# A decoder trunk with two attention branches: when the values of the sliding branch are transposed, and when the modulation row sums run

## The chip, the cores and the metric

The kernel runs on one core of one Trainium2 chip, in one launch. The metric is the device time of that launch in microseconds (us); less is better. Comparisons are made between medians of several runs on the same chip.

The core has several engines that run side by side, each with its own queue in order: TensorE (PE) multiplies matrices and transposes, VectorE (DVE) and ScalarE (ACT) do element-wise work, GpSimd (POOL) does small jobs and issues some transfers, SyncE (SP) issues most transfers. An engine waits at an instruction until the semaphores that it names have arrived, and everything behind it on that engine waits too.

## The reference

D_MODEL = 1024, 512 positions, one layer, fp32. In outline:

```python
cs = silu(c)
mod = cs @ w_ada + b_ada                      # 6 rows of 1024: shift1, scale1, gate1, shift2, scale2, gate2
h = rmsnorm(x, norm1_g) * (1 + scale1) + shift1
qa, ka, va, qd, kd, vd, ga, gd = split(h @ w_in)
out_a = sliding_window_attention(qa, ka, va)  # 8 heads of 64, 2 kv heads, window 128, sinks, ALiBi
out_d = diff_attention(qd, kd, vd)            # 4 heads: (softmax_1 - lam * softmax_2) @ v, then rmsnorm per head
merged = sigmoid(ga) * (out_a @ w_branch_swa) + sigmoid(gd) * (out_d @ w_branch_diff)
x = x + gate1 * (merged @ w_out)
h2 = rmsnorm(x, norm2_g) * (1 + scale2) + shift2
x = x + gate2 * conv_ffn(h2)                  # up, causal conv of width 3, gelu, gate, down
return rmsnorm(x, final_g)
```

The rows shift1 and scale1 of `mod` are needed at the very start. The other four (gate1, shift2, scale2, gate2) are needed after the attentions only.

## The kernel before

**Stages.** From 0 to about 60 us the kernel computes shift1 and scale1, the first norm and the first six column blocks of the projection. Then follow the sliding attention (60 to 125 us), the differential attention (125 to 225 us), the gates, branches, merge and output projection, and the MLP with its norm. An fp32 product is made of three fp32r matmuls (`mm3`, L118 to L121): each operand is split into a high part (a copy on ACT, L115 or L430) and a low part (a subtraction on DVE, L116 or L431).

**Order on PE.** The order of PE's work is written out by hand (`manual_schedule`). `fill(n)` (L495) puts n ticks of projection work between the steps of the attentions. A tick is one k slice of a projection: three 128x512 matmuls, 0.23 us each from start to start. `SWA_FILL` and `DIFF_FILL` say how many ticks go where. The order on DVE and ACT is chosen when the program is built, from priorities and estimated times; the softmaxes and the evacuations of transposes have a high one (`HP`). Once built, each engine keeps that order.

**Sliding attention.** Four pairs of heads; for pair i: `swa_scores(i, 0)` and `swa_scores(i, 2)` (first and last two blocks of 128 queries; L563 adds the bias and takes the row maxima on DVE), `swa_softmax` (exponentials on ACT, scaling L586 on DVE), `swa_transpose(i, 0)` and `(i, 1)` (L598, two groups each, every group into a bank of PSUM), `swa_values`. `turn_va` (L448) transposes the values of this branch on PE and evacuates them as high and low part.

**Differential attention.** 16 steps s = (h, n): head h, query block n, whose scores span (n + 1) x 128 keys. `diff_scores` (reductions L680), `diff_softmax` (exponentials L694, reciprocal L697, scalings L699, L700), `diff_transpose` (L709, evacuated to `aTh` and `aTl` by L430 and L431). The scores of blocks 0 and 1 of a head are made together, and their softmaxes are asked for one behind the other. At block 0 of the next head come the values of the head before (`diff_values`), and some ticks behind these the statistics of its norm (`pss`, `rt`, with a power on POOL at L175) and their spread (`rb`, L739, multiplied in by L740).

**The tag "t".** Two banks of PSUM with the tag "t" are shared in turn by `pva`, the transposes `tp`, `td` and `pv`, the norm's `pss` and `rb`, and the row's `pr`.

**The modulation rows.** `ada_rows` (L750) makes the four later rows in halves of 512, so eight of them, each in four steps. A step is one load of 512 KB (`ra`, L757, on SP's queue, in one of four buffers `raw` that weight loads share) and two sums on DVE (`arow`, L762 or L764: 128 x 512 times a column of `cs`, plus what is there). After the fourth step the sums are split (`arh` on ACT, `arl` on DVE, L116), and one tick later `ada_spread` adds up the 128 partitions by two matmuls on PE (`pr`), copies the row on ACT and writes it to memory by a transfer of POOL. The next row's first sum waits for that transfer, as the row has one buffer. `fill` takes a step at every eighth tick, from tick 8 on, whatever stage runs. After tick 20 (`ADA_EASY`) the sums have half of the high priority.

Of the kernel before, what the change touches and what calls it, by code (L numbers as in the profile page):

```python
# [11 lines left out]
ALU = mybir.AluOpType  # L12
# [15 lines left out]
HP = 100000  # L28
ST = 6
ADA_LAG = 1  # L30
ADA_EVERY = 8
ADA_EASY = 20
ADA_START = 4
V_LAG = 13
STAT_LAG = 10
NORM_LAG = 16
SWA_FILL = (2, 2, 5, 2, 2, 2, 2, 3)
# [16 lines left out]
def kernel(  # L54
# [22 lines left out]
    nc = tc.nc  # L77
# [15 lines left out]
    def fbank(name):  # L93
        return bank("f", 2, [P, S], name)
# [4 lines left out]
    def tbank(name, shape=(P, S)):  # L99
        return bank("t", 2, list(shape), name)  # L100
# [4 lines left out]
    def raw_tile(shape, name):  # L105
        return wp.tile(shape, F32, tag="raw", bufs=4, name=name)

    def split_pair(raw, shape, name):
        hi = wp.tile(shape, F32R, tag="whi", bufs=WB, name=name + "_h")
        lo = wp.tile(shape, F32R, tag="wlo", bufs=WB, name=name + "_l")  # L110
        split(hi, lo, raw)
        return hi, lo
# [314 lines left out]

    def evac(hi, lo, src, scale=None):
        if scale is None:
            nc.scalar.copy(hi, src)  # L430
            nc.vector.tensor_sub(lo, src, hi.bitcast(F32))  # L431
        else:
            nc.scalar.activation(hi, src, AF.Copy, scale=scale)
            nc.vector.scalar_tensor_tensor(lo, src, scale, hi.bitcast(F32), ALU.mult, ALU.subtract)
# [3 lines left out]
    def evac_q(i):  # L438
        evac(qa[:, i, 0], qa[:, i, 1], acc6[i], qsc[:, i : i + 1])
# [8 lines left out]
    def turn_va():  # L448
        pv = tbank("pva")
        for t in range(NT):  # L450
            nc.tensor.transpose(pv[:, t * P : (t + 1) * P], vT[:, t * P : (t + 1) * P], ident)
        pv3 = pv.rearrange("p (t d) -> p t d", t=NT)
        for a, cc in ((0, 0), (64, 192)):
            evac(va[:, 0, :, cc : cc + 64], va[:, 1, :, cc : cc + 64], pv3[:, :, a : a + 64])
# [20 lines left out]
    def load_cols(src, col, name):  # L475
        r = raw_tile([P, KT, P], name)
        nc.sync.dma_start(r, src[:, col : col + P].rearrange("(a p) n -> p a n", p=P))
        return split_pair(r, [P, KT, P], name)
# [9 lines left out]
    current, tick = [], [0]  # L488

    def prefetch():  # L490
        while units and len(loaded) < 2:
            load, run = units.pop(0)
            loaded.append((load(), run))

    def fill(n):  # L495
        for _ in range(n):
            if not current:
                prefetch()
                if loaded:
                    wts, run = loaded.pop(0)  # L500
                    current.append(run(wts))
                    if tick[0]:
                        prefetch()
            if tick[0] == 7:
                prefetch()
            if current:
                try:
                    next(current[0])
                except StopIteration:
                    current.clear()  # L510
            for e in list(later):
                e[0] -= 1
                if e[0] <= 0:
                    later.remove(e)
                    e[1]()
            tick[0] += 1
            if tick[0] >= ADA_START and tick[0] % ADA_EVERY == 0:
                next(ada, None)

    def after(n, fn):  # L520
        later.append([n, fn])

    def steps(o, wts, rhs, nk, k0=0, cl=slice(0, P)):
        wh, wl = wts
        for k in range(nk):
            mm3(o, wh[:, k, cl], wl[:, k, cl], rhs[0][k0 + k], rhs[1][k0 + k], k == 0, k == nk - 1)
            if k < nk - 1:
                yield
# [59 lines left out]
    def swa_transpose(i, j):  # L588
        c = pairs[i]
        ph = ap.tile([P, 1024], F32R, tag="aTh", bufs=2, name=f"pTh{i}_{j}")  # L590
        pl = ap.tile([P, 1024], F32R, tag="aTl", bufs=2, name=f"pTl{i}_{j}")
        for b in range(2):
            wb = 512 if b == 0 else 384
            tp = tbank(f"tp{i}_{j}_{b}")
            for m in range(wb // P):
                kb, n = 2 * b + m // 2, 2 * b + m // 2 + m % 2
                off = (kb - max(0, n - 1)) * P
                nc.tensor.transpose(tp[:, m * P : (m + 1) * P], c.sb[n][:, j, off : off + P], ident)  # L598
            with tc.high_priority(offset=HP):
                evac(ph[:, b * 512 : b * 512 + wb], pl[:, b * 512 : b * 512 + wb], tp[:, :wb])  # L600
        c.pT.append((ph, pl))

    def swa_values(i):
# [80 lines left out]
            scored[s] = mx, pm  # L684

    def diff_softmax(s):
        with tc.high_priority(offset=HP):
            h, n = divmod(s, NT)
            slope = 2.0 ** (-2 * (h + 1))
            mx, pm = scored[s]  # L690
            lsum = ap.tile([P, 2], F32, tag="dls", bufs=3, name=f"dls{h}_{n}")
            nc.vector.tensor_scalar_mul(mx, mx, -slope)  # L692
            for m in range(2):
                nc.scalar.activation(  # L694
                    pm[m], pm[m], AF.Exp, bias=mx[:, m : m + 1], scale=slope, accum_out=lsum[:, m : m + 1]
                )
            nc.vector.reciprocal(lsum, lsum)  # L697
            nc.vector.tensor_mul(lsum[:, 1:2], lsum[:, 1:2], nlam)
            nc.vector.tensor_scalar_mul(pm[1], pm[1], lsum[:, 1:2])  # L699
            nc.vector.scalar_tensor_tensor(pm[0], pm[0], lsum[:, 0:1], pm[1], ALU.mult, ALU.add)  # L700
            probs[s] = pm[0]

    def diff_transpose(s):
# [78 lines left out]
    def add_gate_a(j):  # L782
        def gate(wts):
            o = fbank(f"pga{j}")
            yield from steps(o, wts, hT, KT)
            nc.scalar.activation(ta[:, j], o, AF.Tanh, scale=0.5)

        def load():
            if j % 2 == 0:
                r = raw_tile([P, 4, 2 * P], f"wba{j}")  # L790
                for a in range(2):
                    nc.sync.dma_start(
                        r[64 * a : 64 * a + 64],
                        wba[256 * a : 256 * a + 256, j * P : (j + 2) * P].rearrange("(i p) n -> p i n", p=64),
                    )
                pair_w["a"] = split_pair(r, [P, 4, 2 * P], f"wba{j}")
            return pair_w["a"]

        def branch(wts):
            o = fbank(f"pA{j}")  # L800
            rhs = [[outa[b][:, k] for k in range(4)] for b in range(2)]
            yield from steps(o, wts, rhs, 4, cl=slice(j % 2 * P, j % 2 * P + P))
            nc.vector.scalar_tensor_tensor(ta[:, j], ta[:, j], 1.0, o, ALU.add, ALU.mult)

        units.append((lambda: load_cols(win, COL_GA + j * P, f"wga{j}"), gate))
        units.append((load, branch))

    pairs, firsts, scored, probs, aTs = {}, {}, {}, {}, {}
    ada = ada_rows()
    add_head(0)  # L810
    add_head(1)
    fill(SWA_FILL[0])
    swa_scores(0, 0)
    with tc.issue_after(pairs[0].last.ins):
        fill(SWA_FILL[1])
        swa_scores(0, 2)
    with tc.issue_after(pairs[0].last.ins):
        swa_softmax(0)
        fill(1)
        evac_q(3)  # L820
        turn_va()
        fill(SWA_FILL[2] - 1)
    for i in range(SWA_PAIRS):
        more = i + 1 < SWA_PAIRS
        if more:
            swa_scores(i + 1, 0)
        fill(SWA_FILL[3])
        swa_transpose(i, 0)
        fill(SWA_FILL[4])
        swa_transpose(i, 1)  # L830
        if more:
            swa_scores(i + 1, 2)
        fill(SWA_FILL[5])
        if more:
            swa_softmax(i + 1)
        fill(SWA_FILL[6])
        swa_values(i)
        fill(SWA_FILL[7])
# [11 lines left out]
    for s in range(4 * DIFF_HEADS):  # L850
        h, n = divmod(s, NT)
        if n == 0 and 0 < h < 3:
            add_head(h + 1)
        elif s == 12:
            add_gate_a(2)
            add_gate_a(3)
        fill(DIFF_FILL[1])
        nxt = {0: (), 1: (s + 1,), 2: (s + 1,), 3: (s + 1, s + 2)}[n] if s < 15 else ()
        if nxt:
            diff_scores(*nxt)  # L860
        fill(DIFF_FILL[2])
        diff_transpose(s)
        for z in nxt:
            diff_softmax(z)
        if n == 0 and h:
            diff_values(h - 1)
            fill(DIFF_FILL[3])
    for j in range(4, KT):
        add_gate_a(j)
    fill(1)  # L870
# [653 lines left out]
    e = cbuf[1][:, 1024:2048].rearrange("p (t n) -> p t n", n=S)  # L1524
# [269 lines left out]
```

## Time and profile before

| | |
|---|---|
| time, median of 3 runs | 715.93 us (714.68 to 716.32) |
| the profiled execution's own time | 716.59 us |
| its span in the trace | 714.5 us |
| mean granted clock of PE | 0.993 |
| PE busy | 688.4 us (96%) |
| weight loads of PE (PEld) | 603.0 us (84%) |
| DVE busy | 588.5 us (82%) |
| ACT busy | 384.2 us (54%) |
| row sums L764 | 56 of 748 ns, 41.9 us in all |
| loads `ra` | 32 of 512 KB, 4.2 us from issue to landing (median) |

How to read it: busy time is the time in which an engine has an instruction in work, and PE's matmuls are pipelined, so that one that is recorded as 0.39 us long starts 0.23 us after the one before. The span is shorter than the execution's time by 2.1 us, which lie around it. In a row of the timeline stand start, duration, engine, line, operation, out<-in, tile, shape, count, and in brackets how long the engine had been idle before and what released it. In windows and waits, idle time of an engine counts only where another waits for it.

### The profile page before, as it was taken

The numbers are of one execution on the slowest core, as the hardware profiler recorded it, in microseconds if no ns is written. First come the engines' busy times: TensorE is split into PE (matmuls) and PEld (weight loads), VectorE is DVE, ScalarE is ACT, GpSimd is POOL, SyncE is SP. The second block draws the span as 40 slices with busy tenths as digits, with TensorE's granted clock in tenths as the row PEclk, the third lists the DMA queues.
The fourth block names the chain that finished last, engine by engine and source line by source line (L and its number), as shares of the span: only waits on it lengthen the run. The fifth ranks groups of instructions, "written<-read, shape, count | busy, mean of one in ns | idle before, by whom it ended". The sixth has DMA issues, their size and how long they took to land. (4 is left out here: it accounts for less than half of the span.)

```text
span 714.5 us, 11275 instructions
## 1 busy us (share of the span) xinstructions
PE 688.4 (96%) x4187; PEld 603.0 (84%) x4187; DVE 588.5 (82%) x1125; ACT 384.2 (54%) x677; POOL 84.4 (12%) x101
## 2 busy tenths in 40 slices
PE   5999899999999999999999999999999999999994
PEld 5777778777787888888879999999999999888884
DVE  5998978797986774865479899888889899979996
ACT  3646566455554233432258666555555666656664
POOL 4000000001000100000012021111111102540300
PEclk9999999999999999999999999999999999999998
DMA  9983522453553664737717598877789738996903
GB/s 307 293 264 96 173 64 83 148 163 102 151 159 105 225 196 140 235 118 210 232 59 148 153 201 203 191 185 217 190 199 229 164 123 233 182 203 194 160 0 119
DMA packets 115863, 121.82 MB, mean 170 GB/s; under 512 B 4415, under 2 KB 93280, under 8 KB 115808
## 3 DMA queue, kind: packets, MB, share of 16 engines
q1 hardware_dynamic: 96894, 95.09, 42.1%
q0 software_dynamic: 18720, 25.73, 21.2%
q8 instruction: 33, 0.54, 0.3%
q10 hardware_dynamic: 194, 0.28, 0.1%
q14 instruction: 22, 0.18, 0.1%
HBM read 118.97 MB, written 2.11 MB: 169 GB/s over the span
## 5 line engine op out<-in xcount | busy, mean ns | idle before, releaser
L1133 PE MATMUL up<-t,m_whi 128*128 128x256 f32 x528 | 96.1, 283 | 0.0
L1133 PEld LDWEIGHTS up<-t,m_whi 128*128 128x128 f32 x528 | 82.3, 192 | 0.0
L1133 PE MATMUL up<-t,m_wlo 128*128 128x256 f32 x264 | 74.7, 283 | 0.1
L1133 PE MATMUL up<-bh,p_wlo 128*128 128x256 f32 x232 | 65.7, 284 | 0.6 <-DVE p_wlo L1076 0.6
L1133 PE MATMUL up<-bh,p_whi 128*128 128x256 f32 x232 | 65.6, 283 | 0.0
L1133 PE MATMUL up<-bl,p_whi 128*128 128x256 f32 x232 | 65.6, 283 | 0.0
L1133 PEld LDWEIGHTS up<-t,m_wlo 128*128 128x128 f32 x264 | 50.6, 192 | 0.3 <-DVE m_wlo L1076 0.3
L1133 PEld LDWEIGHTS up<-bh,p_wlo 128*128 128x128 f32 x232 | 44.4, 192 | 1.1 <-DVE p_wlo L1076 1.1
L1133 PEld LDWEIGHTS up<-bh,p_whi 128*128 128x128 f32 x232 | 44.5, 192 | 0.0
L1133 PEld LDWEIGHTS up<-bl,p_whi 128*128 128x128 f32 x232 | 44.5, 192 | 0.0
L1044 POOL DMA_DIRECT2D s<-in_w_up_dram x21 | 27.2, 1385 | 143.0 <-DMA s<-in_w_up_dram 92.7
L764 DVE SCALAR_TENSOR_TENSOR arow<-ra,cs,arow 128x512 f32<-128x512 f32 x56 | 41.9, 748 | 1.4 <-DMA ra<-in_w_ada_dram 0.7
L1076 DVE TENSOR_TENSOR m_wlo<-s,m_whi 128x1024 fp32r<-128x1024 f32 x31 | 37.7, 1216 | 2.0 <-ACT m_whi L1072 2.0
L1072 ACT CAST m_whi<-s 128x1024 fp32r<-128x1024 f32 x31 | 32.5, 1047 | 9.3 <-DVE s L1066 5.9
L1133 PE MATMUL up<-t,p_whi 128*128 128x256 f32 x176 | 32.2, 283 | 0.0
L175 POOL TENSOR_TENSOR r<-ms,mhalf 128x1 f32<-128x1 f32 (+1 forms) x16 | 13.4, 838 | 144.7 <-DVE ms L173 77.2
L694 ACT ACTIVATE sd<-sd,dmx 128x128 f32<-128x128 f32 (+3 forms) x32 | 17.8, 556 | 22.0 <-DVE dmx L692 15.4
L777 POOL DMA_DIRECT2D mod_rows<-arow x8 | 4.3, 540 | 200.5 <-ACT arow L776 200.3
L1133 PEld LDWEIGHTS up<-t,p_whi 128*128 128x128 f32 x176 | 27.4, 192 | 0.2 <-issue 0.2
L1140 ACT ACTIVATE gT<-a,cv 128x512 f32<-128x512 f32 x22 | 17.7, 813 | 17.6 <-DVE a L1175 17.3
L1072 ACT CAST p_whi<-wa 128x1024 fp32r<-128x1024 f32 x18 | 18.7, 1042 | 12.0 <-PE up L1133 10.8
L1133 PE MATMUL up<-t,p_wlo 128*128 128x256 f32 x88 | 24.9, 283 | 0.0
(485 smaller groups left out, 2119.5 us busy)
## 6 DMA issues: line engine op xcount, KB each, us to landing
ra<-in_w_ada_dram SPq DMA_DIRECT2D x32, 512.0 KB, 4.2
wa<-in_w_up_dram SPq DMA_DIRECT2D x22, 512.0 KB, 4.6
s<-in_w_up_dram SPq DMA_DIRECT2D x21, 512.0 KB, 5.0
s<-in_w_up_dram POOLq DMA_DIRECT2D x21, 512.0 KB, 6.5
adaw<-in_w_ada_dram SPq DMA_DIRECT2D x16, 512.0 KB, 5.1
w<-in_w_in_dram SPq DMA_DIRECT2D x12, 512.0 KB, 3.9
a<-in_w_up_dram SPq DMA_DIRECT2D x11, 512.0 KB, 4.7
b<-in_w_down_dram SPq DMA_DIRECT2D x10, 512.0 KB, 3.9
```

The costliest lines, as they stand in the source:

```text
L175: nc.gpsimd.tensor_tensor(r0, ms, mhalf[:, :n], ALU.pow)
L694: nc.scalar.activation(pm[m], pm[m], AF.Exp, bias=mx[:, m : m + 1], scale=slope, accum_out=lsum[:, m : m + 1])
L764: nc.vector.scalar_tensor_tensor(ac, r[:, a], cc, ac, ALU.mult, ALU.add)
L777: nc.gpsimd.dma_start(mod_rows[idx : idx + 1, hf * S : (hf + 1) * S], row)
L1044: nc.gpsimd.dma_start(dst, upblock(*blk), accum_op=ALU.add)
L1072: nc.scalar.copy(W[J, name][0], R[J, SRC[name]])
L1076: nc.vector.tensor_sub(lo, R[J, SRC[name]], hi.bitcast(F32))
L1133: nc.tensor.matmul(o[u], w[:, k, cu], b[:, k], start=name in ("p1", "m5", "p2") and k == 0 and x == 0, stop=k == 3 and x == 2, skip_group_ ...
L1140: nc.scalar.activation(grow(j), av[J][:, u], AF.Identity, bias=cv[:, 66 + j : 67 + j], scale=cv[:, 44 + j : 45 + j])
```

## The change

Three things are changed. First, `turn_va` stands between the two first score blocks of the sliding attention, one tick behind the first, where it stood behind the first softmax; the tick 7 prefetch of weights is replaced by one that is issued behind the first pair's transposed probabilities (`pairs[0].turned`, the copy on ACT). Second, the steps of `ada_rows` are held back until the differential attention: no step is taken while `hold` is set, which it is during the sliding attention and at the blocks n = 2 and 3 of a head. At n = 0 and 1 a step is taken every 4 ticks, and after the differential attention every 6. A step taken at a tick issues its load and enters its two sums into DVE's work; where these come in DVE's order is decided at the build. Third, the softmax of block 1 of a head is issued behind the last exponential and the last multiplication of block 0's (`issue_after`).

No matmul, transpose, sum or load is added or removed in number.

```diff
--- before.py
+++ after.py
@@ -28,9 +28,9 @@
 HP = 100000
 ST = 6
 ADA_LAG = 1
-ADA_EVERY = 8
+ADA_EVERY = 4
+ADA_LATE = 6
 ADA_EASY = 20
-ADA_START = 4
 V_LAG = 13
 STAT_LAG = 10
 NORM_LAG = 16
@@ -427,8 +427,9 @@
 
     def evac(hi, lo, src, scale=None):
         if scale is None:
-            nc.scalar.copy(hi, src)
+            ins = nc.scalar.copy(hi, src)
             nc.vector.tensor_sub(lo, src, hi.bitcast(F32))
+            return ins
         else:
             nc.scalar.activation(hi, src, AF.Copy, scale=scale)
             nc.vector.scalar_tensor_tensor(lo, src, scale, hi.bitcast(F32), ALU.mult, ALU.subtract)
@@ -501,8 +502,6 @@
                     current.append(run(wts))
                     if tick[0]:
                         prefetch()
-            if tick[0] == 7:
-                prefetch()
             if current:
                 try:
                     next(current[0])
@@ -514,8 +513,12 @@
                     later.remove(e)
                     e[1]()
             tick[0] += 1
-            if tick[0] >= ADA_START and tick[0] % ADA_EVERY == 0:
+            waits[0] += 1
+            if not hold[0] and waits[0] >= every[0]:
+                waits[0] = 0
                 next(ada, None)
+
+    waits, hold, every = [0], [True], [ADA_EVERY]
 
     def after(n, fn):
         later.append([n, fn])
@@ -597,7 +600,7 @@
                 off = (kb - max(0, n - 1)) * P
                 nc.tensor.transpose(tp[:, m * P : (m + 1) * P], c.sb[n][:, j, off : off + P], ident)
             with tc.high_priority(offset=HP):
-                evac(ph[:, b * 512 : b * 512 + wb], pl[:, b * 512 : b * 512 + wb], tp[:, :wb])
+                c.turned = evac(ph[:, b * 512 : b * 512 + wb], pl[:, b * 512 : b * 512 + wb], tp[:, :wb])
         c.pT.append((ph, pl))
 
     def swa_values(i):
@@ -684,20 +687,24 @@
             scored[s] = mx, pm
 
     def diff_softmax(s):
-        with tc.high_priority(offset=HP):
+        with tc.high_priority(offset=HP), ExitStack() as order:
             h, n = divmod(s, NT)
+            if n == 1:
+                for e in ends[s - 1]:
+                    order.enter_context(tc.issue_after(e.ins))
             slope = 2.0 ** (-2 * (h + 1))
             mx, pm = scored[s]
             lsum = ap.tile([P, 2], F32, tag="dls", bufs=3, name=f"dls{h}_{n}")
             nc.vector.tensor_scalar_mul(mx, mx, -slope)
             for m in range(2):
-                nc.scalar.activation(
+                exp = nc.scalar.activation(
                     pm[m], pm[m], AF.Exp, bias=mx[:, m : m + 1], scale=slope, accum_out=lsum[:, m : m + 1]
                 )
             nc.vector.reciprocal(lsum, lsum)
             nc.vector.tensor_mul(lsum[:, 1:2], lsum[:, 1:2], nlam)
             nc.vector.tensor_scalar_mul(pm[1], pm[1], lsum[:, 1:2])
-            nc.vector.scalar_tensor_tensor(pm[0], pm[0], lsum[:, 0:1], pm[1], ALU.mult, ALU.add)
+            end = nc.vector.scalar_tensor_tensor(pm[0], pm[0], lsum[:, 0:1], pm[1], ALU.mult, ALU.add)
+            ends[s] = exp, end
             probs[s] = pm[0]
 
     def diff_transpose(s):
@@ -805,20 +812,21 @@
         units.append((lambda: load_cols(win, COL_GA + j * P, f"wga{j}"), gate))
         units.append((load, branch))
 
-    pairs, firsts, scored, probs, aTs = {}, {}, {}, {}, {}
+    pairs, firsts, scored, probs, aTs, ends = {}, {}, {}, {}, {}, {}
     ada = ada_rows()
     add_head(0)
     add_head(1)
     fill(SWA_FILL[0])
     swa_scores(0, 0)
     with tc.issue_after(pairs[0].last.ins):
-        fill(SWA_FILL[1])
+        fill(1)
+        turn_va()
+        fill(SWA_FILL[1] - 1)
         swa_scores(0, 2)
     with tc.issue_after(pairs[0].last.ins):
         swa_softmax(0)
         fill(1)
         evac_q(3)
-        turn_va()
         fill(SWA_FILL[2] - 1)
     for i in range(SWA_PAIRS):
         more = i + 1 < SWA_PAIRS
@@ -826,6 +834,9 @@
             swa_scores(i + 1, 0)
         fill(SWA_FILL[3])
         swa_transpose(i, 0)
+        if i == 0:
+            with tc.issue_after(pairs[0].turned.ins):
+                prefetch()
         fill(SWA_FILL[4])
         swa_transpose(i, 1)
         if more:
@@ -854,6 +865,7 @@
         elif s == 12:
             add_gate_a(2)
             add_gate_a(3)
+        hold[0] = n > 1
         fill(DIFF_FILL[1])
         nxt = {0: (), 1: (s + 1,), 2: (s + 1,), 3: (s + 1, s + 2)}[n] if s < 15 else ()
         if nxt:
@@ -865,6 +877,7 @@
         if n == 0 and h:
             diff_values(h - 1)
             fill(DIFF_FILL[3])
+    hold[0], every[0] = False, ADA_LATE
     for j in range(4, KT):
         add_gate_a(j)
     fill(1)
```

## The prediction

> **What bounds the kernel now.** I read the first page of the profile from the top: busy times, the tenths of the 40 slices, the chain that ended last.
>
> ```profile
> PE 688.4 (96%) x4187; PEld 603.0 (84%) x4187; DVE 588.5 (82%) x1125; ACT 384.2 (54%) x677; POOL 84.4 (12%) x101
> ...
> PE 40%; DVE 5%; issue 1%; ACT 1%; POOLq 0%; DVEq 0%; ACTq 0%
> ```
>
> TensorE (PE) is busy 96% of the 714.5 us span, and it is the largest entry of the chain, though most of the chain's share is not put down to any engine, so I do not lean on it alone. VectorE (DVE) with 82% is close behind. The change takes no instruction away and adds none that counts: the program of after has the same matmuls, transposes and sums, in other places. So it can only act through time in which PE waits. I therefore asked for PE's waits next (columns: engine, line, what it waited for, us in total, times, longest).
>
> ```profile
> PE tp L598 <- DVE pTl L431: 2.9, 2, 2.1
> ...
> PE td L709 <- DVE sd L700: 1.8, 4, 1.1
> ...
> PE od L120 <- DVE aTl L431: 0.5, 1, 0.5
> ```
>
> The waits I leave out of this list belong to the first 60 us or to the MLP, which the change does not reach. 2.9 + 1.8 + 0.5 = 5.2 us is thus the most that can be won. Where these lie, and how loaded DVE is there, is read from windows of 20 us (length, busy PE, PEld, DVE, ACT, POOL, each with its count, then granted clock, DMA share, GB/s) and from the timeline of PE.
>
> ```profile
> 60.00:80.00 20.00, 17.91 (x116) 13.84 (x115) 17.32 (x60) 10.25 (x30) 0.00 (x0) 1.00 0.35 107
> 140.00:160.00 20.00, 18.90 (x103) 14.56 (x100) 17.38 (x48) 11.00 (x24) 0.51 (x1) 1.00 0.45 133
> 180.00:200.00 20.00, 19.76 (x109) 15.40 (x108) 18.79 (x50) 11.48 (x26) 1.55 (x1) 1.00 0.54 158
> 260.00:280.00 20.00, 20.00 (x90) 16.54 (x89) 12.54 (x17) 5.78 (x8) 0.54 (x1) 1.00 0.68 211
> ```
>
> ```profile
> 72.06 0.60 PE L598 MATMUL tp<-ident,st 128*128 128x128 f32 x4
> 74.76 0.55 PE L598 MATMUL tp<-ident,st 128*128 128x128 f32 x3 [2.09 <-DVE pTl L431]
> ...
> 91.68 1.01 PE L598 MATMUL tp<-ident,st 128*128 128x128 f32 x7 [0.81 <-DVE pTl L431]
> ...
> 153.11 0.30 PE L709 MATMUL td<-ident,sd 128*128 128x128 f32 x1 [1.10 <-DVE sd L700]
> ...
> 172.84 0.63 PE L709 MATMUL td<-ident,sd 128*128 128x128 f32 x4 [0.17 <-DVE sd L700]
> ...
> 197.62 0.63 PE L709 MATMUL td<-ident,sd 128*128 128x128 f32 x4 [0.24 <-DVE sd L700]
> ```
>
> While the attentions run (60 to 225 us) DVE has 1 to 5 us of room in 20, and PE is fed just in time: the transposes of a fourth block wait 0.17 and 0.24 us, so any work put ahead of them on DVE is paid almost at once. After 240 us DVE has 5 to 8 us of room in 20 and PE waits for nothing there. A loss made before it is therefore not recovered later, and a gain is kept.
>
> **The sliding attention.** Before, the transposed values (`pva`) and the first group of probability transposes hold both banks of tag "t", so the second group waits 2.09 us for L431. After, the values are transposed a tick and more earlier, the second group finds a bank, and the third has to wait for the first group's low half instead. PE would want the third group 1.77 us after the second (76.53 − 74.76), that is at 72.06 + 0.47 + 1.77 = 74.3. On DVE the two row sums at 69.61 and 70.13 (0.40 and 0.67 start to start) are gone, but the add at 71.78 waited for ACT's exponentials, not for them; behind it stand the reductions, four scalings, a low half of 0.6 that now comes first, and the 0.6 itself: 74.4 to 75.1, plus 0.14 until PE starts (74.62 to 74.76). So 0.3 to 1.0 us of the 2.09 stay; I take 0.5: gain 1.6. The 0.81 of the second stall goes with the sums ahead of it. At the third pair the sums restart with two at once, ahead of its score reductions; its transposes were just in time, and I charge 0.4 (bounds 0 and 1.3, two sums). Net: −1.6 − 0.8 + 0.4 = **−2.0** (bounds −2.9 and 0).
>
> **The differential attention.** A row takes four steps of two sums. Steps now come every fourth tick while n is 0 or 1. No step is issued at n = 2, 3, but the engines keep the order of the program, not its times. In after's program the two sums of a row's fourth step stand on DVE behind the score reductions of block 3 and ahead of its softmax, and in the heads 1 and 2 the row's low split `arl` stands ahead of the last multiplication (L700) too. Their 512 KB load was issued at n = 1, but behind weight loads in SP's queue, and its buffer comes free late. A sum is 0.66 us start to start, `arl` 0.60, a weight's low split 1.14. Head by head:
> - Head 0, block 0: a step's two sums wait for their load and precede the first reductions, which move from 127.88 to about 129.5. The transposes had some 0.8 us of room: +0.75 (bounds 0 and 1.6).
> - Head 1, block 0: the 1.10 at 153.11 came from sums interleaved with the softmaxes of two blocks; the first softmax now ends before the second begins, and the sums are behind it: −1.1 (bounds −1.1 and 0).
> - Head 1, block 3. Before, the reciprocal at 171.03 followed ACT's exponentials after 0.16 idle. After, two sums and a 0.6 low half that before lay in the same place fill the stretch, and the softmax ends with `arl` in it: 0.7 late at the reciprocal and 0.6 more at `arl`, less the little room: +1.2 (bounds 0 and 1.9, two sums and `arl`).
>
> ```profile
> 165.80 0.16 DVE L183 TENSOR_TENSOR rt<-r 128x4 f32<-128x4 f32 x1 [0.94 <-POOL r L175]
> ...
> 171.03 0.17 DVE L697 RECIPROCAL dls<-dls 128x2 f32<-128x2 f32 x1 [0.16 <-ACT sd L694]
> ...
> 178.08 0.69 DVE L740 TENSOR_TENSOR of<-of,rb 128x512 f32<-128x512 f32 x1 [0.17 <-PE rb L739]
> ```
>
> - Heads 2 and 3, block 0: the row's spread `pr` now takes a bank of tag "t" between `rb` and these transposes, so they need `rb`'s own bank, which L740 frees (0.6 us from its start) behind a softmax. Before, `td` came at once after `rb`. +0.6 each, 1.2 (bounds 0 and 1.8).
> - Head 2, block 3: as in head 1, with a weight's split among the sums: +1.3 (bounds 0 and 3.0: 1.32 + 0.60 + 1.14).
> - Head 3, block 3: before already has a sum and `arl` here; after has one low half more ahead of L700: +0.5 (bounds 0 and 1.3).
> - Last values (L120, 0.46 before): `aTl` now stands behind one weight split more: +1.1 (bounds 0 and 1.2).
>
> Together 0.75 − 1.1 + 1.2 + 1.2 + 1.3 + 0.5 + 1.1 = **+4.95**.
>
> **The rest, at nothing.** After the loop a step comes every 6 ticks, a row every 24 (some 17 us at 0.69 us a tick); load, sums, splits and spread chain to 12 to 17 us. Before, `arl` was done about 7 us ahead of its spread; a cover of 2 to 5 us remains by this count. If it went, it would cost a few tenths a row. The early `prefetch` issues the same loads in the same order on SP. The added order on DVE and ACT at n = 1 holds back only the second softmax, and its transposes come 6 ticks (4 us) later.
>
> **The sum.** −2.0 + 4.95 = +2.95 us. The profiled execution took 716.59 us, of which 714.5 is span; it stood 0.66 above the median 715.93. 716.59 + 2.95 = 719.5, less 0.66: **718.9 us**. A change of 0.2% (1.4 us) is about what a measurement of this kernel can tell.
>
> [...] Here PEld in the stretches without waits is 16.5 of 20 us, and it falls to 13.84 between 60 and 80, 2.7 short, where the waits listed add up to 2.1. [...]
>
> **Rivals.**
> - *The stalls go and none comes* (0.16). The sliding attention gains 2.0 and head 1 gains 1.1: 716.59 − 3.1 − 0.66 = 712.8 us. It decides at block 3: if the fourth step's loads have landed early enough that its sums run while DVE waits for ACT or POOL (0.94 at 165.80 is such a gap), they cost nothing. For it: DVE has 16 to 19 us busy of 20, not 20. Against: the sums stand behind the reductions whenever the load lands, and the gap at 171.03 is only 0.16.
> - *The stalls move* (0.12): the gain of 3.1 as above, and half of the seven new terms (6.05), 716.59 − 3.1 + 3.0 − 0.66 = 715.8 us: no difference.
> - *The change does not do what it says*: sums still run beside blocks 2 and 3. The order bears that out, so it is part of the forecast. Were it otherwise, the terms 1.2, 1.3, 0.5 would fall away, and 715.9 would be left, in the case above.
> - *PE's clock falls* (0.02). The granted clock is 1.00 in the windows that hold the waits of 2.09 and 1.10, so waits of this size do not touch it. My largest new term is 1.3. Two of them in one would be like the 2.09, so I price it by a window in which PE ran at half speed for as long as it waits now, 3 us: 722. The Trainium skill (TensorE: Matmul & The Clock Gate, "What's actually happening") puts the fall after an idle window of about 3.4 us, which no wait here reaches.
>
> **How the numbers follow.** The forecast has 0.70. Slower: it and the clock, 0.72; same 0.12; faster 0.16. The range reaches down to 714.4, where the second rival and a part of the first (new terms at a quarter) lie, and up to 722.6: the forecast with 3.7 more, about half of what its upper bounds would add. The likeliest case's own range is 717.4 to 722.6.
>
> **What would show it.** In the trace of after: the 2.09 wait gone and one below 1.1 at the third group; none of 0.81 near 91; the wait at head 1's first block gone, and waits of 0.5 to 1.5 us in front of block 3's transposes (L716) in heads 1 and 2, with two `arow` and `arl` between the reductions and L706 on DVE. PE's waits in the differential stretch should sum to about 7 us instead of 2.3. Wrong: these transposes wait no longer than before, the list of waits of PE is shorter than 5.2 us, or waits appear after 240 us.

## The result: slower by 11 us

| | before | after |
|---|---|---|
| median | 715.66 us (4 runs, 714.68 to 716.32) | 726.91 us (4 runs, 725.68 to 727.39) |
| ratio | | 1.0151, 95% interval 1.0129 to 1.0174 |
| span of the profiled execution | 714.5 us | 723.5 us |

The change makes the kernel slower, as forecast, but by 11.2 us, where 3.0 us were forecast and the range ended at 722.6 us.

The first page for after. As before, PE has 4187 matmuls. Its busy share is the same in per cent, and nothing here tells where 9 us went.

```profile
PE 693.2 (96%) x4187; PEld 603.6 (83%) x4187; DVE 589.0 (81%) x1125; ACT 383.6 (53%) x677; POOL 83.0 (11%) x101
```

PE's waits in after (columns as in the prediction; waits of the first 60 us, of the MLP and below 0.5 us are left out):

```profile
PE td L716 <- DVE sd L706: 3.2, 3, 1.2
PE tp L601 <- DVE pTl L431: 2.5, 2, 1.8
...
PE pr L780 <- ACT arh L115: 1.9, 1, 1.9
...
PE od L120 <- DVE aTl L431: 1.3, 1, 1.3
...
PE td L716 <- DVE of L747: 0.9, 2, 0.4
...
PE pr L781 <- DVE arl L116: 0.6, 2, 0.3
```

The transposes of probabilities (`tp`) wait as long in sum as before, in another place. `td` and `od` wait longer. The spread of the rows, `pr`, is new in the list, with 2.5 us. Windows of after show a second loss that no list of waits shows (the last three columns are granted clock, DMA share, GB/s):

```profile
220.00:240.00 20.00, 17.39 (x80) 13.98 (x79) 9.29 (x15) 8.85 (x16) 1.11 (x2) 0.91 0.30 82
...
260.00:280.00 20.00, 17.87 (x70) 13.78 (x69) 13.94 (x19) 5.22 (x7) 0.97 (x2) 0.91 0.69 211
```

The granted clock was 1.00 in all windows of before from 60 to 320 us. Here it falls twice. Finer windows show the first fall:

```profile
226.00:228.00 2.00, 1.03 (x4) 0.95 (x5) 1.51 (x3) 0.00 (x0) 0.00 (x0) 0.89 0.86 255
228.00:230.00 2.00, 2.00 (x10) 2.00 (x9) 0.00 (x0) 0.07 (x1) 0.00 (x0) 0.50 0.66 216
230.00:232.00 2.00, 2.00 (x8) 1.55 (x8) 0.00 (x0) 1.10 (x2) 0.00 (x0) 0.76 0.08 32
232.00:234.00 2.00, 2.00 (x12) 1.61 (x11) 0.00 (x0) 0.00 (x0) 0.00 (x0) 1.00 0.00 0
```

The share of clock that is missing in these windows adds up to 1.70 us (0.22 + 1.00 + 0.48), which is 3.4 us at half speed. The slow stretch stands right behind the waits of 1.06, 0.28 and 1.26 us at 223 to 227 us. The second fall stands at 274 to 280 us, with 0.84, 0.50 and 0.81 in its windows, behind the wait of 1.90 us. The rows of PE's timeline in after that the prediction's steps spoke of:

```profile
73.88 1.01 PE L601 MATMUL tp<-ident,st 128*128 128x128 f32 x7 [0.76 <-DVE pTl L431]
...
104.28 1.01 PE L601 MATMUL tp<-ident,st 128*128 128x128 f32 x7 [1.78 <-DVE pTl L431]
...
171.17 0.63 PE L716 MATMUL td<-ident,sd 128*128 128x128 f32 x4 [0.92 <-DVE sd L706]
...
198.04 0.63 PE L716 MATMUL td<-ident,sd 128*128 128x128 f32 x4 [1.24 <-DVE sd L706]
...
223.59 0.63 PE L716 MATMUL td<-ident,sd 128*128 128x128 f32 x4 [1.06 <-DVE sd L706]
...
273.57 0.49 PE L780 MATMUL pr<-arh,onesr 128*128 128x512 f32 x1 [1.90 <-ACT arh L115]
```

The next table gives, for one instruction of PE in both timelines, its start in after minus its start in before:

| instruction | after − before | so the stretch up to it costs |
|---|---|---|
| first sliding scores | −1.21 | −1.21 (startup, see below) |
| first differential scores | −1.79 | −0.58 |
| values of the last head, L119 | +2.08 | +3.87 |
| spread of head 2's norm (`rb`, 229.28 before) | +4.48 | +2.40 (0.80 wait at L120, the rest the first fall) |
| spread of head 3's norm (`rb`, 245.39 before) | +4.58 | +0.10 |
| end of the span | +9.0 | +4.42 (2.47 waits of `pr`, the rest the second fall and small gaps) |

The two medians stand 11.2 us apart and the two profiled executions 9.1. The startup's 1.2 is part of that difference; about 0.9 us is left unexplained. The startup is not touched by the change, and it differs mostly because before's own profile has a fall of the clock there, which after's has not:

```profile
14.00:16.00 2.00, 0.89 (x4) 0.89 (x5) 1.78 (x11) 1.01 (x4) 1.36 (x2) 0.74 1.11 336
16.00:18.00 2.00, 2.00 (x12) 2.00 (x11) 1.93 (x7) 0.00 (x0) 0.00 (x0) 0.50 1.08 342
18.00:20.00 2.00, 1.57 (x10) 1.25 (x10) 2.00 (x6) 1.43 (x3) 0.00 (x0) 0.91 1.10 342
```

It follows waits of PE of 2.75 us (at 12.62) and 1.15 us (at 15.11). From 15.11 to 19.40 before takes 4.29 us; the same instructions take 2.94 us in after (14.40 to 17.34).

### The profile page after: what moved, and what is told of

Read it like the earlier page. It is cut to its first block, busy times and chain, and to the rows that moved or that the text cites. A ratio compares the mean times of both kernels' runs of the same rounds, so it can differ in the third digit from the quotient of the medians.

```text
span 723.5 us, 11275 instructions
## 1 busy us (share of the span) xinstructions
PE 693.2 (96%) x4187; PEld 603.6 (83%) x4187; DVE 589.0 (81%) x1125; ACT 383.6 (53%) x677; POOL 83.0 (11%) x101
```

## Experiments

Two theories stood against each other. The first: the loss is a sum of single waits (loads, sums, splits ahead of something that PE needs), and of falls of the clock that follow some of them. The second: VectorE is late as a whole, and a wait that is taken away turns up again.

Each median is followed by its ratio to the runs of before on the same chip, with the 95% interval. Where a run is set against after, the two ratios are subtracted and the difference is taken of 715.66 us; with the intervals of both, such a figure is uncertain by some 2 us.

### The part that carries the loss

**Rows only (e7).** Before with the second of the three changes alone:

```diff
-ADA_EVERY = 8
+ADA_EVERY = 4
+ADA_LATE = 6
...
+        hold[0] = n > 1
         fill(DIFF_FILL[1])
```

> Kernel before with the steps of the rows where after has them (held until the differential attention, every 4 ticks at blocks 0 and 1, every 6 behind it); values and softmax order as before. Theory: this part alone carries the loss: waits of about 4 us more in the differential stretch, 2.5 us at pr behind it, and one or two falls of the clock: 724 to 728 us. Rival: the loss comes from the parts together, and this one alone is 4 us or less slower than before.

Measured: 727.11 us, 1.0139 (1.0117 to 1.0161). Within the intervals the rows' new places carry the whole loss (after has 1.0151). At head 1's first block, where before waited 1.10 us, PE does not wait at all in this kernel, although the softmax order is the old one.

**Order only (e6).** Before with the second block's softmax behind the first's:

```diff
+            if n == 1:
+                for e in ends[s - 1]:
+                    order.enter_context(tc.issue_after(e.ins))
```

> Kernel before with the second block's softmax issued behind the first's; nothing else. Theory: the wait of 1.10 us at head 1's first block falls to 0.3, as it did in after, so 0.8 less: 714 us. Rival: that wait came from row sums on VectorE between the two softmaxes, which stay in this kernel: no change, 714.8 us.

Measured: 719.59 us, 1.0052 (1.0037 to 1.0068): slower, against both expectations. At head 1's first block PE now waits 1.97 us, and 1.75 us at head 3's block 3:

```profile
155.95 0.30 PE L713 MATMUL td<-ident,sd 128*128 128x128 f32 x1 [1.97 <-DVE dmx L695]
```

With the softmaxes one behind the other, two sums and a weight split stand between the first one's reciprocal and its last multiplication (152.66 to 155.45 us in e6's DVE timeline). So the wait of 1.10 us is cured by taking the sums away from there, as e7 shows, and not by the order. The profile of e6 also has two falls of the clock, at 74 to 80 and 156 to 162 us, behind waits of 2.13 and 1.97 us.

**Turned values only (e5).** Before with `turn_va` and the prefetch moved:

```diff
-        fill(SWA_FILL[1])
+        fill(1)
+        turn_va()
+        fill(SWA_FILL[1] - 1)
         swa_scores(0, 2)
```

> Kernel before with the values transposed between the first scores (and the prefetch that goes with it); row sums and softmax order as before. Theory (the parts act by their own waits): the wait of 2.09 us at the second transpose group shrinks by 0.7 to 1.4 us, the rest stays: 714 us, 0.7 to 1.4 less than before. Rival (the sums beside the sliding attention make that wait, not the bank): the wait stays near 2 us and the time is before's.

Measured: 714.89 us, 0.9986 (0.9974 to 0.9997). The waits of 2.09 and 0.81 become 1.00 and 0.96: 0.9 us in the trace, 0.8 in the medians. The step on the bank of `pva` holds.

**Turn and order (e8).** Both of the two edits above, with the rows as before.

> Kernel after with the rows' steps as before (every 8 ticks from tick 8, no hold). Theory: the gains of the two other parts add up: 1.5 to 2.2 us less than before, 713 us, and no wait over 1 us after 60 us. Rival: with the sums back beside the sliding attention nothing is won, 715 us, or some of after's loss shows here too.

Measured: 717.23 us, 1.0027 (1.0016 to 1.0038). The rival's second half came: −1.0 and +3.7 us from the ratios of e5 and e6 would make +2.7, and +1.9 was measured.

### What in the rows' places costs

**No fourth sums (e13).** After without the two sums of the fourth step in the first four half rows, which so lack a quarter of their terms:

```diff
-                        for a in range(2):
+                        for a in range(0 if k == 6 and idx < 2 else 2):
```

> Kernel after without the two sums of the fourth step in the first four half rows (the loads stay; these rows lack a quarter of their terms, that is what is left out). With them the row's split leaves block 3 as well. Theory (these sums and the split ahead of block 3's softmax make its waits): the waits of 0.92, 1.24 and 1.06 us in front of block 3's transposes fall to 0.3 or less each, some 2.5 us in all; the rest of after's loss stays. Rival (VectorE is behind as a whole in the differential attention): the waits shrink by less than half.

Measured: 723.8 us, 1.0102 (1.0079 to 1.0125). Block 3's waits fall from 3.2 to 1.7 us:

```profile
PE td L716 <- DVE sd L706: 1.7, 3, 0.6
```

That is 1.5 us less, just under half, so by the letter it is the rival's figure: these sums and the split make half of the waits. The other half stays without them. Where it comes from was followed in one head only: in e13 the weight split `wba_l` runs ahead of block 2's last scaling instead, and head 2's block 3 begins its reductions at 192.05 us where after began them at 190.88. DVE's timeline of after shows what the sums did in head 2's block 3:

```profile
192.10 0.74 DVE L771 SCALAR_TENSOR_TENSOR arow<-ra,cs,arow 128x512 f32<-128x512 f32 x1
...
193.44 0.74 DVE L771 SCALAR_TENSOR_TENSOR arow<-ra,cs,arow 128x512 f32<-128x512 f32 x1
...
194.18 1.21 DVE L116 TENSOR_TENSOR wba_l<-wba,wba_h 128x1024 fp32r<-128x1024 f32 x1
195.31 0.55 DVE L431 TENSOR_TENSOR aTl<-td,aTh 128x384 fp32r<-128x384 f32 x1
195.78 0.15 DVE L703 RECIPROCAL dls<-dls 128x2 f32<-128x2 f32 x1
195.85 0.67 DVE L116 TENSOR_TENSOR arl<-arow,arh 128x512 fp32r<-128x512 f32 x1
```

ACT had the exponentials ready at 194.55; the reciprocal that needs them starts 1.2 us later, behind a weight split and a low half that the two sums have pushed back, and `arl` puts 0.6 us more ahead of the scalings.

**Three steps a head (e14).** After with one number changed:

```diff
-ADA_EVERY = 4
+ADA_EVERY = 5
```

> Kernel after with ADA_EVERY = 5: three steps a head, so that the program has no sum at all in head 3's block 3, but two to four sums still in the blocks 3 of heads 1 and 2. Theory: the wait in front of head 3's block 3 (1.06 us in after) goes, those of heads 1 and 2 stay near 1 us or grow; with fewer steps done by then the last rows end later, and some tenths are lost behind them. Time 725 to 728 us. Rival (it is the number of sums in the stage, not their place): all three waits shrink alike.

Measured: 727.36 us, 1.0163 (1.0134 to 1.0191). In head 3's block 3 there is no sum, and PE does not wait; in heads 1 and 2 four and five sums stand in that block, and PE waits 1.95 and 2.24 us:

```profile
PE td L716 <- DVE sd L706: 4.2, 2, 2.2
```

What decides is how many sums stand in block 3, not how many the stage has: no sum in block 3 gives 0 to 0.6 us (e14's head 3, e13), two sums 0.9 to 1.2 (after), four or five 1.9 to 2.2 (e14). The delay of head 3 is not all gone, though: PE waits 1.91 us at the last values behind it (1.26 + 0.28 in after).

**Sums behind the sliding attention (e10).** After, with an order for the sums:

```diff
+                            with tc.issue_after(pairs[SWA_PAIRS - 1].last.ins):
```

> Kernel after with every row sum issued behind the last score reduction of the sliding attention, so that none stands in front of a score reduction there. Theory: the 1.78 us at the third pair came from a sum on VectorE that waited for its load (0.58 idle) ahead of the third pair's reductions; it goes, 1.8 us less than after (725.1 us), if the sums find room later. Rival: the sums that ran there are pushed into the differential attention, where VectorE has no room, and the waits there grow by as much: 727 us or more.

Measured: 723.54 us, 1.0111 (1.0092 to 1.0131), 2.9 us less than after. The 1.78 us at the third pair goes, as the theory has it, and 0.79 us comes at the fourth. The waits in the differential attention stay as they were (0.33, 0.90, 0.43, 1.24, 0.42, 1.06), so the rival falls. The two profiled executions stand further apart (721.73 against 725.68 us), and most of that is that the clock falls nowhere from 60 to 320 us in this profile; whether the edit or chance kept it up was not shown. Why the sum stood there in after at all: `hold` delays the step's place in the program, not its place on DVE. Nothing made the sums wait for the sliding attention, so they were placed in it when the program was built:

```profile
99.36 0.75 DVE L771 SCALAR_TENSOR_TENSOR arow<-ra,cs,arow 128x512 f32<-128x512 f32 x1 [0.58 <-DMA ra<-in_w_ada_dram]
100.03 0.68 DVE L431 TENSOR_TENSOR outal<-oa,outah 128x512 fp32r<-128x512 f32 x1
100.63 0.74 DVE L771 SCALAR_TENSOR_TENSOR arow<-ra,cs,arow 128x512 f32<-128x512 f32 x1
101.29 0.28 DVE L566 CUSTOM_DVE_ANT_0 st<-sw,dsw 128x128 f32<-128x128 f32 x1
```

PE was done with the scores of the fourth pair at 98.7, and their reductions begin at 101.29. In between a sum waited for its load, and two sums and a low half ran. The weight split and the low halves that the transposes need stand behind all that.

**Late steps every 8 ticks (e9).** After with `ADA_LATE`:

```diff
-ADA_LATE = 6
+ADA_LATE = 8
```

> Kernel after with ADA_LATE = 8: behind the differential attention a step every 8 ticks, as in before, instead of every 6. Theory (a row's chain of load, sums and split is longer than the ticks allow): 2 ticks more between the fourth load and the spread take the waits of pr away (2.5 us) and the fall of the clock behind them (1.7): 4.2 us less than after, some 722.7 us. Rival (the spread is late because its load waits in SP's queue behind weight loads, and a longer stage only moves that): the waits at pr stay above 1.5 us; or the rows end too late for the output projection, and 2 us or more are lost there.

Measured: 723.89 us, 1.0110 (1.0088 to 1.0132). All waits at `pr` go, and so does the fall of the clock at 275 us. In their place come 0.68 us at a branch weight and 0.98 at the output projection. The last row is spread at 329 us instead of 309, but that this makes these two waits is not shown: e1 has both too, with its last row at 301. Of the 4.2 us hoped for, 2.9 came.

**The spread later (e2).** After with `ADA_LAG` 5 instead of 1.

> Kernel after, with the row's spread 5 ticks behind the split instead of 1. Theory: the waits of pr for arh and arl late (1.9 + 0.34 + 0.23 = 2.5 us) go, and with them the fall of the clock behind the 1.9 (1.7 us): about 4.2 us less than after, some 722.7 us. Rival: the row has one buffer, so the next row's sums start later by the same 4 ticks and are as late at the next spread: no change, 726.9 us.

Measured: 732.0 us, 1.0242 (1.0216 to 1.0267): 6.5 us above after, worse than the rival. The row's buffer is free later, DVE's first sum waits for it (2.03 us at 220.42 in its timeline), and the sums bunch up in block 3, where PE waits 2.8, 2.9 and 4.3 us.

### The clock, and the end of the attention

**Last values later (e1).** After with more work ahead of them:

```diff
-    fill(1)
+    fill(5)
     diff_values(DIFF_HEADS - 1)
```

> Kernel after, with 5 ticks instead of 1 between the last transposes and the last head's values. Theory (waits and the clock): the waits of 0.28 and 1.26 us in front of the last values go, and with them the fall of the granted clock right behind them (1.7 us lost): about 3.2 us less than after, some 723.7 us, and the clock stays at 1.00 between 220 and 240 us. Rival (VectorE is late as a whole and only hands the wait on): the low half of the last probabilities is as late, the wait turns up at the next reader, and the time stays within 1 us of after's 726.9.

Measured: 720.07 us, 1.0069 (1.0057 to 1.0081), 5.9 us less than after, nearly twice the theory's 3.2. The waits of 0.28 and 1.26 and the first fall go as expected. So do the 2.5 us at `pr` and the second fall, which the theory left in; 1.4 us come at a branch weight and 0.7 at the output projection.

**Both later (e3).** e1 and e2 together.

> Kernel after, with both edits: 5 ticks ahead of the last values and the spread 5 ticks behind the split. Theory: both gains add up, 3.2 + 4.2 = 7.4 us less than after, some 719.5 us, and no window after 60 us with a granted clock under 1.00. Rival: one wait takes the place of the other, and less than 4 us is gained.

Measured: 730.1 us, 1.0215 (1.0201 to 1.0229). As e2 already costs 6.5 us by itself, adding up was not tested.

**Dummy matmuls (e4).** After with matmuls that fill the wait and are thrown away:

```diff
+        if h == DIFF_HEADS - 1:
+            for k in range(8):
+                nc.tensor.matmul(o, t[:, 4, 0:P], hTh[0], start=True, stop=True)
```

> Kernel after, with 8 matmuls of 128x512 whose result is thrown away put ahead of the last values (8 x 0.227 = 1.8 us of work where PE waits 1.54 us). This tells the clock from the wait. Theory (the clock falls for want of PE activity): the clock does not fall at 227 us, 1.7 us less, and the dummies cost 1.8 - 1.54 = 0.3: some 1.4 us less than after, 725.5 us. Rival (what is lost there is the wait alone, or the clock falls for another reason): the clock falls as before and the time is 0.3 us above after's.

Measured: 726.32 us, 1.0155 (1.0142 to 1.0169). The clock stays at 1.00 at 227 us, and from head 3's block 3 to the spread of head 2's norm PE takes 8.59 us where after took 10.17. But it falls at 104 us behind the wait at the third pair (0.93 between 100 and 125 us), where it did not fall in after. By itself this run settles nothing, because e7, e9 and e10 keep the clock at 1.00 there without dummies, with the same three waits as in after (1.06, 0.28 and 1.26 or 1.27 us).

These runs give the clean price of a fall instead. Between L119 of the last values and the spread of head 2's norm, after and e9 run the same instructions with the same waits. After takes 233.76 − 225.20 = 8.56 us and e9 takes 234.28 − 227.29 = 6.99. The one with the fall is 1.57 us longer. (e7 and e10, without a fall, take 6.98.)

### Mended versions

**After mended (e15).** e10's edit, `ADA_EVERY = 5`, and `fill(3)` ahead of the last values.

> Kernel after with three edits: sums behind the sliding attention's last reductions, ADA_EVERY = 5, and 3 ticks ahead of the last values. Theory (the losses add up): 3.4 us from the first edit as in its own run, 0.8 to 1.1 from head 3's block 3, 1.5 from the last values with the clock kept up: 720 us. Rival: the waits at the spreads behind the loop grow by what is won, 724 us.

Measured: 724.68 us, 1.0114 (1.0089 to 1.0139). The rival's time came, and half of its mechanism: the waits at `pr` did not grow, but they are still 2.5 us, in other rows. Besides, the 4.2 us in block 3 of heads 1 and 2 that belong to `ADA_EVERY = 5` came with it, and one fall of the clock behind the first of them.

**Turned values, 3 ticks ahead of the last values (e11).** e5 with `fill(3)`.

> Kernel before with the turned values of after and 3 ticks instead of 1 ahead of the last values; rows as before. Theory: the 0.46 us in front of the last values goes too, and the time is 0.4 us below that of the turn alone: 714.2 us where before is at 715.3. Rival: the ticks are missing later, no change against the turn alone.

Measured: 714.1 us, 0.9980 (0.9965 to 0.9995). This is faster than both kernels. Against the turn alone (0.9986) it can't be told apart: the 0.46 us at the last values goes, and 0.6 comes at the first gate behind them, as the rival has it.

**Low priority for the sums (e12).** e5 with `ADA_EASY = 100000`.

> Kernel before with the turned values of after and the row sums at plain priority all the time, so that the softmaxes and splits go first on VectorE. Theory (sums ahead of a softmax make the waits of the differential attention): the 1.1, 0.5 and 0.3 us there go, 2 us less than the turn alone, some 713 us. Rival: the sums then come late for their spreads, PE waits at pr, and the time is above before's.

Measured: 714.78 us, 0.9989 (0.9977 to 1.0001). Head 1's block 3 does not wait any more (0.54 in e5), head 2's waits 0.82 (0 in e5). The wait moves, and none comes at `pr`, so neither expectation was met.

**No step at n = 3 (e16).** e11 with `hold[0] = n == 3` and steps every 8 ticks otherwise.

> The version of turned values and 3 ticks ahead of the last values, with no step taken while n = 3. Theory: a step less near block 3 takes 0.5 us of its waits, 713.5 us. Rival: a step that is not taken at n = 3 shifts the others onto n = 0, where the wait of 1.1 us already is: 715 us or more.

Measured: 716.27 us, 1.0011 (0.9996 to 1.0027). The waits in block 3 of heads 1 and 3 become 0.16 and 0, but that of head 2 becomes 1.88 us: five sums now stand there, so a step that is put off by a few ticks lands its sums in the next tight place.

So neither theory holds alone: single waits can be taken away (e1, e9, e10), but in e12, e15 and e16 part of what was taken away came back in another place.

## Why the prediction was right or wrong

The direction was right, and in the differential attention the waits were found where the steps put them. What failed: the third pair was priced too low (+0.4, measured +1.95), the row spreads behind the loop stood under "the rest, at nothing" (measured 2.47), and the falls of the clock were no term of the sum (two in after's profile, 1.57 us each). The table has the steps in us, forecast and measured as waits of PE in after minus before. That the sum meets the 9.0 us of the spans is partly luck: the startup is 1.2 us shorter in the profile of after, mostly because of before's fall there, and small gaps that no wait shows make about as much.

| step | forecast | measured |
|---|---|---|
| first stall of the sliding attention | −1.6 | −1.33 (0.76 left) |
| second stall | −0.8 | −0.81 |
| third pair | +0.4 (0 to 1.3) | +1.95 |
| head 0, block 0 | +0.75 | 0 |
| head 1, block 0 | −1.1 | −0.77 |
| head 1, block 3 | +1.2 | +0.75 |
| heads 2 and 3, block 0 | +1.2 | +0.85 |
| head 2, block 3 | +1.3 | +1.00 |
| head 3, block 3 | +0.5 | +0.73 |
| last values | +1.1 | +1.08 |
| row spreads behind the loop | 0 | +2.47 |
| falls of the clock | 0 | 2 falls, 1.57 each (measured for the first, taken for the second) |
| sum | +2.95 | +9.1 |

- **The differential attention was right.** The seven steps sum to 4.95 us, measured are 3.64, all within their bounds. That sums in block 3 make waits is shown by e13 and e14, and e13 puts their part, with the split, at half; the rest is open. Head 0's block 0 cost nothing: its reductions start 1.05 us later behind the scores than in before (127.14 − 123.25 against 127.88 − 125.04), and the room there took it. In head 1's block 0 the right thing happened for a reason that I only half had: I credited the softmax order and the sums' place, and e6 and e7 show that the place alone does it, and that the order harms as long as the sums stay in their old places.
- **The third pair was mis-sized.** I priced two sums, 1.3 us at most. What I left out is that a sum can stand at the head of DVE's queue waiting for its own load (0.58 us) while ready reductions stand behind it: 0.58 and two sums of 0.66 make 1.90, close to the 1.95 measured. e10 shows it. (The bounds given for the whole sliding attention, −2.9 and 0, are wider than its terms add up to, −2.6 and −0.6.)
- **"A cover of 2 to 5 us remains by this count" failed.** By its own figures a row of 17 us and a chain of 12 to 17 leave 0 to 5 us, not 2 to 5. Nor would a late row cost "a few tenths": the spread at 273.57 us waits 1.90 at `arh` and 0.23 at `arl`. Its last load is issued 6.06 us before PE asks for the split at 271.67 (273.57 − 1.90), and takes most of that to land:

```profile
265.61 0.37 SPq L764 DMA_DIRECT2D ra<-in_w_ada_dram  x1
...
270.86 0.75 DVE L771 SCALAR_TENSOR_TENSOR arow<-ra,cs,arow 128x512 f32<-128x512 f32 x1 [0.96 <-DMA ra<-in_w_ada_dram]
```

It took 5.2 us (the median in before is 4.2), and DVE stood idle 0.96 us for it. When PE asks, the second sum has not begun (272.12). With 2 ticks a step more, in e9, no spread waits. The prediction's own sign of being wrong, waits after 240 us, is these.
- **The rival on the clock was wrong twice.** It took the granted clock of 1.00 beside a wait of 2.09 us in one execution as a bound, and gave a fall 0.02. Waits of that size are followed by a fall in some executions and not in others, so one execution without a fall is no evidence that none comes. And the profile that it was read from had a fall, at 14 to 20 us, behind a wait of 2.75 us and one of 1.15. It also took one wait at a time: the fall at 227 us followed three waits that together make 2.6 of 4.4 us. The Trainium skill (TensorE: Matmul & The Clock Gate, "What's actually happening") says that the clock is set by how busy PE was recently, in a window of about 3.4 us that runs free of the kernel. The 3.4 us at half speed agree with this, and so does it that the same wait is followed by a fall in one execution and not in another. The idle window of about 3.4 us ahead of a fall that the same section of the Trainium skill gives, and the prediction cites, is not borne out: waits of 1.87 to 2.46 us were enough in nine places of these runs.
- **"The change does not do what it says" was true.** The rival's own price rested on block 3 alone, and the part that cost was beside the sliding attention.
- **The short weight loads between 60 and 80 us** pointed at nothing beyond the wait: with the stall at 74.76 us shortened to 0.76 the window of 60 to 80 us has 15.15 of PEld, up 1.3, about what the waits there fell by (2.09 − 0.76).

## What to carry to other kernels

Work that is moved out of one place lands in another: look up, for each instruction that is moved, whose queue it will stand at the head of, whether its own load will be there, and what is ready behind it. An edit that holds back the issue of a step in the program does not hold back its place on an engine whose order a scheduler chooses; in e10 an order edge did. Where a matrix engine has no slack, count several small waits within a few microseconds together, since a fall of the clock behind them can cost more than each (here 1.57 us behind waits of 1.06, 0.28 and 1.26).

## What the runs showed of the hardware

- Of 24 waits of PE of 1.6 to 2.7 us in dense stretches (profiles of all runs but e2, after the first 60 us), 9 were followed by a fall of the clock and 15 were not: 2.09 (before), 2.24 (e14) and 2.71 us (e3) without, 1.87 (e9), 1.96 (e13) and 1.98 us (e8) with. The same wait in the same place went both ways (at the third pair 1.95 us in e1 without, 1.94 in e4 with). The three waits of 1.06, 0.28 and 1.26 us were followed by a fall in after and not in e7, e9 and e10.
- A fall cost 1.57 us in the stretch compared; the granted clocks of 0.89, 0.50 and 0.76 in three windows of 2 us make 0.22 + 1.00 + 0.48 = 1.70. The windows of every other fall after 60 us add up to 1.70 too, but for one of twice that (3.42, e2, behind a wait of 4.32 us).
- Spreads of some us between executions of one kernel (after 725.68 to 727.39) are of this size. The mean granted clock is known for every execution: over 73 executions of before in four batches, each taken against the mean of its batch, time and clock have a correlation of −0.60. So about a third of the variance goes with the clock. How many falls each execution had is not shown, as only one execution of each kernel was profiled.
